# A gMLP value projection by seven block products on two sets of three PSUM banks, with modulation steps moved to the FFN in-projections

## The chip, the cores and the metric

The kernel runs on one core of one Trainium2 chip. The metric is the device time of one execution in microseconds; the time before is the median of three runs.

## The reference

A two-layer generator over 512 latent and 256 context tokens, width 1024. Each layer is FFN, token mixer, FFN; every sublayer is modulated by shift, scale and gate and closed by a LayerNorm over the residual. Layer 0 mixes by a chunked gMLP, layer 1 by attention. What the change touches is the gMLP's `v` and the modulation:

```python
def modulation(cond, w_mod, b_mod):            # 9 vectors of 1024 per layer and condition
    m = jax.nn.silu(cond) @ w_mod + b_mod
    return jnp.split(m[..., None, :], N_MOD, axis=-1)

def ffn_sublayer(x, shift, scale, gate, w_in, w_out, ln_g, ln_b):
    y = swiglu(modulate(x, shift, scale), w_in, w_out)
    return layer_norm(ALPHA * x + 0.5 * gate * y, ln_g, ln_b)

def gmlp_mix(h, w_in, sgu_g, sgu_b, w_s, b_s, w_out):       # h: 768 x 1024, w_in: 1024 x 6144
    b_, t_, _ = h.shape
    u, v = jnp.split(jax.nn.gelu(h @ w_in, approximate=False), 2, axis=-1)
    v = layer_norm(v, sgu_g, sgu_b)
    v = v.reshape(b_, t_ // CHUNK, CHUNK, GMLP_GROUPS, GMLP_HALF // GMLP_GROUPS)
    v = jnp.einsum('gpq,bnqgc->bnpgc', w_s, v) + b_s.T[None, None, :, :, None]
    return (u * v.reshape(b_, t_, GMLP_HALF)) @ w_out
```

Both conditions (latent and context) need the modulation vectors, save the last four of layer 1, which only the latent tokens use.

## The kernel before

*Stages.* One instruction stream per engine runs six sublayers one after another: the first FFN (to about 540 us of the profiled execution), the gMLP (to 1190: the v projection from 555.97 to 753.86, then u with the spatial gate, then the out-projection), the second FFN (to 1698), the third, of layer 1 (to 2200), attention, and the last FFN on the latent tokens. The 768 tokens are six blocks of 128.

*Products.* Every operand is split into two fp32r parts, high and low, and a product is three matmuls: high by high, high by low, low by high. The FFN in-projections work on half the tokens (three blocks) and half the width at a time and take seven such block products where eight are the plain count (`tile_strassen`, L1024; matmuls 128x384). Their stationary operands are the boxes `comb` named B11, B21, T1, T2, T3, B22, T4: B11 and B21 are the two halves of the width of blocks 0 to 2, B22 belongs to blocks 3 to 5, the T are differences. `combine` (L670) makes all but the first two in pieces, between the first products of a sublayer. Sums of weights are made on DVE ahead of the split (`units`, L304).

*The v projection before* is plain: `gmlp` (L1217) calls `token_proj` (L1172) for six chunks of 512 columns; each takes 8 slices of the width by 6 blocks by 3, 864 matmuls of 128x512 in all, in six banks. `evacuate` then runs gelu on ACT, `bn_stats` on DVE and a DMA to `v_spill` on POOL's queue.

*Weights.* `weight_order` (L207) lists all pieces of 256 KB in the order of use. `load_raw` (L277) issues them on SP's queue as one of six raw tiles comes free. ACT casts a piece to its high part, DVE subtracts for the low one (`split_later` L170, `flush` L175); up to eight split pieces wait (`w`), and `pump` (L347) decides how many are prepared at a slot between products.

*Modulation.* `mod_unit` (L387) makes one of the 18 vectors in 16 steps (two halves of 512 columns, eight slices of the width). A step takes a raw piece `mraw` of 256 KB (SP, three tiles) and runs one DVE `scalar_tensor_tensor` per condition into `acc`. After the eighth step of a half, POOL runs a `partition_all_reduce` (L410) and a DMA that adds the row in DRAM (L411), once per condition. `MOD_PLAN` (L69) says which vectors belong to which sublayer; `fill` (L526) runs one step at a slot of the products, and `fill_pair` (L538) two where there is one condition. What is left when the slots are over is run at once at the start of `End.begin` (L1941), which closes a sublayer. In the FFN's in-projection, tiles from `OPENED` on have one `fill_pair`, every fourth two.

*The closing.* In the last products of an out-projection, block after block is finished: DVE adds and `bn_aggr` to `ve`, POOL raises it to the power -1/2 (`rs`, L203), DVE makes `nb`, ACT the normalised `z`. PE transposes block b-2 after six of the 18 matmuls of block b, so block 0 is turned while block 2 is multiplied. PE, like each engine, runs its instructions in the order written.

Of the kernel before, what the change touches and what calls it, by code (L numbers as in the profile page):

```python
# [7 lines left out]
F32 = mybir.dt.float32  # L8
F32R = mybir.dt.float32r
AF = mybir.ActivationFunctionType  # L10
# [59 lines left out]
    [(0, 2), (0, 3), (0, 4)],  # L70
    [(0, 5), (0, 6), (0, 7), (0, 8), (1, 0), (1, 1)],
    [(1, 2), (1, 3)],
    [(1, 4), (1, 5), (1, 6), (1, 7)],
# [20 lines left out]
class Backbone:  # L94
# [112 lines left out]
    def weight_order(self):  # L207
# [96 lines left out]
    def units(self, jobs):  # L304
        dve, w = self.dve, None
        for kind, srcs in jobs:
            if kind == "u":
                for _ in srcs:
                    w = self.unit_of(self.take())
                    self.drop(1)  # L310
                    yield w
                continue
            g1 = self.take()
# [31 lines left out]
            yield w  # L345

# [323 lines left out]
    def combine(self):  # L670
# [14 lines left out]
        h1, h2, t1, t4 = [], [], [], []  # L685
        for n in range(HALF):
            b = HALF + n
            banks = [self.h_transposes(b, half) for half in range(int(begun is not None), 2)]
            h2.append(cut(self.z[b][:, 512:1024]))
            if begun:  # L690
                h1.append(begun[n][0])
                t1.append(begun[n][1])
            else:
                h1.append(cut(self.z[b][:, 0:512]))
                self.h_affine(b, 0, banks[0], False, h1[n])
            self.h_affine(b, 1, banks[-1], not begun, h2[n])
# [12 lines left out]
            low("T2", n, t2)  # L709
            if n and not begun:  # L710
                yield
        for name in ("T3",) if begun else ("T1", "T3"):
            self.new_comb(name)
        if not begun:
# [5 lines left out]
            high("T1", 2, t1[2])  # L720
        sub(h1[0], h2[0], h1[0])
# [360 lines left out]
    def ffn(self, l, i, nblocks, end, prev):  # L1082
# [133 lines left out]

    def gmlp(self, l, i, nblocks, end, prev):  # L1217
# [5 lines left out]
        vbox = self.box("v", F32)  # L1223
# [25 lines left out]
        for cc in range(CC):  # L1249

            def evacuate(b, ps):
                v = self.q(512)
                self.act.activation(v, ps, AF.Gelu)
                self.dve.bn_stats(vst[b][:, cc], v)
                nc.gpsimd.dma_start(spill[cc][b * P : b * P + P, :], v)
# [578 lines left out]
    def body(self):  # L1834
# [11 lines left out]
            (self.gmlp, 0, 3, NB, "c"),  # L1846
# [259 lines left out]
```

## Time and profile before

| | us |
|---|---|
| median of three runs (lowest, highest) | 2812.37 (2812.07, 2812.89) |
| the profiled execution, by its own time | 2812.64 |
| span of its instructions | 2810.9 |
| mean granted TensorE clock | 0.998 |
| v projection, in the span | 555.97 to 753.86 |

The page of the profile gives, engine by engine, busy time with its share of the span; then the span in forty equal slices; DMA queues; the chain of work that ended last; and groups of instructions. A row of a timeline reads: start, duration in us, engine, source line, operation, output<-inputs, and in brackets how long the engine was idle before it and which instruction released it. PE is matmul, PEld its weight load, DVE the vector engine, ACT the scalar engine, POOL GpSimd.

### The profile page before, as it was taken

The numbers are of one execution on the slowest core, as the hardware profiler recorded it, in microseconds if no ns is written. First come the engines' busy times: TensorE is split into PE (matmuls) and PEld (weight loads), VectorE is DVE, ScalarE is ACT, GpSimd is POOL, SyncE is SP. The second block draws the span as 40 slices with busy tenths as digits, with TensorE's granted clock in tenths as the row PEclk, the third lists the DMA queues.
The fourth block names the chain that finished last, engine by engine and source line by source line (L and its number), as shares of the span: only waits on it lengthen the run. The fifth ranks groups of instructions, "written<-read, shape, count | busy, mean of one in ns | idle before, by whom it ended". The sixth has DMA issues, their size and how long they took to land.

```text
span 2810.9 us, 40763 instructions
## 1 busy us (share of the span) xinstructions
PE 2768.7 (98%) x14478; PEld 2502.6 (89%) x14478; DVE 2009.0 (71%) x3483; ACT 1245.8 (44%) x2467; POOL 535.2 (19%) x605
## 2 busy tenths in 40 slices
PE   7999999999999999999999999999999999999998
PEld 5999988888899988899999889999988888888886
DVE  6867779587687786687777758777786698733445
ACT  6544432432355532474444237444432666623321
POOL 1001044233311232200102220001242121000001
PEclk9999999999999999999999999999999999999999
DMA  7444366355555464344346534443584524454352
GB/s 232 141 129 123 111 233 202 120 196 195 190 174 165 154 233 144 124 149 143 110 126 204 180 113 131 144 131 116 163 308 154 147 70 89 134 150 132 111 168 82
DMA packets 398820, 430.00 MB, mean 153 GB/s; under 512 B 28504, under 2 KB 288024, under 8 KB 398616
## 3 DMA queue, kind: packets, MB, share of 16 engines
q1 hardware_dynamic: 364504, 319.40, 36.5%
q0 software_dynamic: 34112, 108.00, 12.4%
q8 instruction: 113, 1.85, 0.3%
q14 instruction: 91, 0.75, 0.1%
HBM read 366.10 MB, written 63.41 MB: 153 GB/s over the span
## 4 chain that ended last, share of the span: by engine, by line
PE 65%; ACT 2%; issue 2%; DVE 2%; POOL 1%; DMA 0%; DVEq 0%; POOLq 0%; ACTq 0%; SPq 0%
PE ps L89 64%; PE pp L89 1%; POOL acc L410 0%; ACT z L2004 0%; POOL rs L203 0%; ACT h L628 0%; ACT p L1519 0%; DVE z L89 0%; DVE nm L1511 0%; ACT w L172 0%; ACT comb L642 0%; ACT p L1522 0%; ACT pT L166 0%; POOL zhat L2006 0%; DVE pT L167 0%
## 5 line engine op out<-in xcount | busy, mean ns | idle before, releaser
L89 PE MATMUL ps<-comb,w 128*128 128x384 f32 x5544 | 969.5, 335 | 6.5 <-ACT w L172 3.0
L89 PEld LDWEIGHTS ps<-comb,w 128*128 128x128 f32 x5544 | 961.5, 188 | 10.3 <-DVE w L89 3.8
L89 PE MATMUL ps<-w,acts 128*128 128x512 f32 (+1 forms) x3792 | 860.1, 388 | 0.0
L89 PEld LDWEIGHTS ps<-w,acts 128*128 128x128 f32 x3792 | 707.3, 188 | 145.0
L89 ACT CAST w<-raw 128x512 fp32r<-128x512 f32 x630 | 388.1, 621 | 750.7 <-PE ps L89 657.3
L89 DVE TENSOR_TENSOR w<-raw,w 128x512 fp32r<-128x512 f32 x630 | 459.7, 737 | 313.1 <-ACT w L89 312.2
L89 PE MATMUL ps<-h,w 128*128 128x384 f32 (+2 forms) x2304 | 445.1, 353 | 0.2 <-DVE w L173 0.2
L89 PEld LDWEIGHTS ps<-h,w 128*128 128x128 f32 x2304 | 402.4, 188 | 37.8 <-DVE w L173 0.4
L89 DVE SCALAR_TENSOR_TENSOR acc<-mraw,cs,acc 128x512 f32<-128x512 f32 x378 | 281.4, 778 | 21.0 <-DMA mraw<-in_w_mod_dram 20.5
L89 PE MATMUL ps<-w,h 128*128 128x512 f32 x1200 | 274.6, 390 | 0.0
L410 POOL PARTITION_ALL_REDUCE acc<-acc x56 | 202.7, 3627 | 350.5 <-DVE acc L89 309.2
L89 PEld LDWEIGHTS ps<-w,h 128*128 128x128 f32 x1200 | 224.6, 188 | 46.3
L89 POOL DMA_DIRECT2D act<-stage x84 | 48.0, 571 | 981.1 <-DVE stage L89 950.9
L89 POOL DMA_DIRECT2D q<-act x226 | 128.7, 624 | 456.7 <-DVE acts L89 315.5
L89 DVE TENSOR_TENSOR w<-sums,w 128x512 fp32r<-128x512 f32 x198 | 135.8, 687 | 75.8 <-ACT w L89 75.7
L89 ACT COPY q<-ps 128x384 f32<-128x384 f32 x179 | 86.1, 481 | 205.3 <-PE ps L89 202.0
L89 DVE TENSOR_TENSOR acts<-q,acts 128x384 fp32r<-128x384 f32 (+1 forms) x262 | 146.5, 595 | 9.3 <-ACT acts L89 9.2
L89 ACT CAST acts<-q 128x384 fp32r<-128x384 f32 (+1 forms) x262 | 126.4, 519 | 49.9 <-DMA q<-act 33.9
L89 ACT CAST w<-sums 128x512 fp32r<-128x512 f32 x198 | 122.7, 621 | 31.2 <-DVE sums L323 18.6
L173 DVE TENSOR_TENSOR w<-raw,w 128x512 fp32r<-128x512 f32 x114 | 75.7, 687 | 27.9 <-ACT w L172 27.2
L203 POOL TENSOR_TENSOR rs<-ve,mhalf 128x1 f32<-128x1 f32 (+3 forms) x47 | 39.0, 829 | 273.1 <-DVE ve L200 167.8
L172 ACT CAST w<-raw 128x512 fp32r<-128x512 f32 x114 | 68.2, 632 | 47.3 <-PE ps L89 27.0
(208 smaller groups left out, 2221.6 us busy)
## 6 DMA issues: line engine op xcount, KB each, us to landing
raw<-in_ffn_w_in_dram SPq DMA_DIRECT2D x400, 256.0 KB
mraw<-in_w_mod_dram SPq DMA_DIRECT2D x256, 256.0 KB
raw<-in_ffn_w_out_dram SPq DMA_DIRECT2D x176, 256.0 KB
q<-act POOLq DMA_DIRECT2D x216, 192.0 KB, 4.2
act<-stage POOLq DMA_DIRECT2D x74, 384.0 KB, 3.1
raw<-in_gmlp_w_in_dram SPq DMA_DIRECT2D x96, 256.0 KB
zhat<-z POOLq DMA_DIRECT2D x26, 512.0 KB, 2.9
raw<-in_gmlp_w_out_dram SPq DMA_DIRECT2D x48, 256.0 KB
```

Source lines behind the costliest of these rows:

```text
L89: return self.tc.keep_in_program_order(f(*args, **kwargs))
L172: self.act.copy(hi, src)
L173: self.lows.append((key, lambda: self.dve.tensor_tensor(lo, src, hi.bitcast(F32), ALU.subtract)))
L203: self.last_rstd = self.nc.gpsimd.tensor_tensor(rs, ve, self.mhalf[:, 0:1].to_broadcast([P, n]), ALU.pow).ins
L410: nc.gpsimd.partition_all_reduce(accs[c], accs[c], P, bass_isa.ReduceOp.add)
```

## The change

The v projection becomes `gmlp_v`: the six chunks of columns are taken as three pairs, each pair by seven block products (three blocks by half the width by 512 columns; the products T1, T2, T3, B22, T4 and two more, 36 matmuls of 128x512 each), in two sets of three PSUM banks that take turns. `weight_order` lists its pieces in quads; the new `units_of_pair` forms the sums of weights on DVE. The gMLP is now planned as kind "s", so the FFN before it hands over blocks 0 to 2 as B11 and B21 and `combine` makes the rest while the v stage opens; it also writes the first halves of blocks 3 to 5 to DRAM (`kept`), from which B12 is made for the u projection, which takes its operands from the four boxes. No modulation step runs in the v stage any more: `MOD_PLAN` is divided anew, and the tiles of the FFN in-projections from `OPENED` on take two `fill_pair` each.

```diff
 MOD_PLAN = [
-    [(0, 2), (0, 3), (0, 4)],
-    [(0, 5), (0, 6), (0, 7), (0, 8), (1, 0), (1, 1)],
-    [(1, 2), (1, 3)],
-    [(1, 4), (1, 5), (1, 6), (1, 7)],
+    [(0, 2), (0, 3), (0, 4), (0, 5)],
+    [(0, 6), (0, 7), (0, 8)],
+    [(1, 0), (1, 1), (1, 2)],
+    [(1, 3), (1, 4), (1, 5), (1, 6), (1, 7)],
     [],
     [(1, 8)],
 ]
...
-        for cc in range(GMLP_HALF // 512):
-            o = GMLP_HALF + cc * 512
-            jobs.append(("u", [wi[k * P : k * P + P, o : o + 512] for k in range(KD)]))
+        quad = lambda cc, half: [
+            wi[k * P : k * P + P, GMLP_HALF + cc * 512 : GMLP_HALF + cc * 512 + 512]
+            for k in range(4 * half, 4 * half + 4)
+        ]
+        each = lambda *qs: [s for group in zip(*qs) for s in group]
+        jobs.append(("u", quad(0, 0) + quad(2, 0) + quad(0, 1) + quad(2, 1)))
+        for a in (0, 2, 4):
+            g1, g2, u1, u2 = quad(a, 0), quad(a, 1), quad(a + 1, 0), quad(a + 1, 1)
+            if a < 4:
+                jobs.append(("vr", each(u1, u2, g1) + each(g1, u1) + g2 + u2))
+            else:
+                jobs.append(("vs", g1 + each(u1, u2) + g1 + g2 + each(g1, u1) + g2 + u2))
...
+            if kind[0] == "v":
+                yield from self.units_of_pair(kind == "vr")
...
+    def units_of_pair(self, opened):
+
+        def of_raw():
+            for _ in range(4):
+                w = self.unit_of(self.take())
+                self.drop(1)
+                yield w
+
+        def settled(w):
+            if any(key is w for key, _ in self.lows):
+                self.flush()
+
...
+            s1 = [self.acc() for _ in range(4)]
+            for k in range(4):
+                u1, u2, g1 = self.take(), self.take(), self.take()
+                self.dve.tensor_tensor(s1[k], u1, u2, ALU.add)
+                self.dve.tensor_tensor(held[k], s1[k], g1, ALU.subtract)
+                units.append(self.unit_of(held[k]))
+                self.drop(3)
+                yield units[k]
+            for k in range(4):
+                yield self.unit_of(s1[k])
...
-    def combine(self):
+    def combine(self, keep=False):
...
+                if keep:
+                    self.pool.dma_start(self.kept[n], self.z[b][:, 0:512])
...
-        for name in ("T3",) if begun else ("T1", "T3"):
-            self.new_comb(name)
+        if not begun:
+            self.new_comb("T1")
...
-            self.tile_strassen(lambda: acts.place(f), opened, int(f >= OPENED) * (1 + int(f % 4 == 0)))
+            self.tile_strassen(lambda: acts.place(f), opened, int(f >= OPENED) * 2)
...
+    def gmlp_v(self, room, spill, vst, early_group, late_group):
...
+        self.combining = self.combine(True)
+        sets = [[self.bank(("v", x, t)) for t in range(HALF)] for x in range(2)]
...
+        def finish(cc, b, v):
+            dve.bn_stats(vst[b][:, cc], v)
+            self.nc.gpsimd.dma_start(spill[cc][b * P : b * P + P, :], v)
+
+        def out(cc, b, src):
+            v = self.q(512)
+            act.activation(v, src, AF.Gelu)
+            after.append(lambda: finish(cc, b, v))
...
+        def slot():
+            self.flush()
+            waiting = after[:]
+            after.clear()
+            if todo:
+                todo.pop(0)()
+            elif later:
+                later.pop(0)()
+            if self.combining is not None:
+                self.pump(max(0, min(2, LEAD - len(self.wready))))
+                if next(self.combining, self) is self:
+                    self.combining = None
+            else:
+                self.pump(2)
+            for f in waiting:
+                f()
+
+        def step(x, name, go_on, evacuate):
+            kw = dict(skip_group_check=True) if go_on else {}
+            for k in range(4):
+                (w,) = self.weights(1)
+                while name not in self.made:
+                    next(self.combining, None)
+                c = self.comb[name]
+                for t in range(HALF):
+                    ps, s = sets[x][t], slice(t * P, t * P + P)
+                    self.mm(ps, c[:, 0, k, s], w[:, 0], not go_on and k == 0, False, **kw)
+                    self.mm(ps, c[:, 0, k, s], w[:, 1], False, False, **kw)
+                    self.mm(ps, c[:, 1, k, s], w[:, 0], False, k == 3, **kw)
+                if k == 3:
+                    assert not todo
+                    todo.extend(lambda t=t: evacuate(t, sets[x][t]) for t in range(HALF))
+                slot()
+                self.release(1)
...
+                u2 = zs()
+                step(x, "T2", True, lambda t, ps: act.copy(u2[t], ps))
+                p5 = ms()
+
+                def keep5(t, ps):
+                    act.copy(p5[t], ps)
+                    act.copy(ps, u2[t])
+
+                step(y, "T1", False, keep5)
+            step(x, "T3", True, lambda t, ps: summed(a + 1, HALF + t, ps, p5[t]))
+
+            def third(t, ps):
+                summed(a, HALF + t, ps, p5[t])
+                if tail_seed:
+                    act.copy(ps, tail_seed[t])
+
+            step(y, "B22", True, third)
+            if a == 4:
+                late_group()
+                assert not later
+            step(x, "T4", True, lambda t, ps: out(a + 1, t, ps))
...
+        step(0, "B11", False, lambda t, ps: act.copy(first[t], ps))
+        step(1, "B11", False, lambda t, ps: act.copy(first[3 + t], ps))
+
+        def opened(t, ps):
+            out(0, t, ps)
+            act.copy(ps, first[t])
+
+        step(0, "B21", True, opened)
+        step(1, "B21", True, lambda t, ps: out(2, t, ps))
+        rest(0, 0, first[0:3], first[3:6])
+        rest(1, 2, first[3:6], None)
+        early_group()
+        rest(0, 4, None, None)
...
-            if not cc:
-                self.filler_raw()
-            if cc == CC - 1:
-                load_ws(0)
-                following = group(0)
-                next(following)
-                self.later(4, lambda: next(following))
-            self.pin(cc > 0)
-            self.token_proj(range(NB), evacuate)
...
+        self.gmlp_v(vbox_all, spill, vst, begin_group, lambda: next(self.following))
...
-                self.in_proj(ps, ws, slice(x * HT, x * HT + HT))
+                parts = [self.comb[name] for name in (("B11", "B21"), ("B12", "B22"))[x]]
...
-            (self.gmlp, 0, 3, NB, "c"),
+            (self.gmlp, 0, 3, NB, "s"),
```

Three places in the order of the instructions. In the names, `acc` is a modulation accumulator (in the v stage also a sum of two weight pieces), `mraw` a raw piece of `w_mod`, `cs` the conditioning column, `held` a difference of weight pieces, `vst` the statistics of v, `w` and `raw` split and raw weights, `acts` the FFN's or gMLP's activations, `q` scratch.

First, DVE near the end of the gMLP's out-projection, up to the first instruction of the closing (L778 before, L852 after). Before:

```order
L89 SCALAR_TENSOR_TENSOR acc<-mraw,cs,acc 128x512 x2
L89 TENSOR_TENSOR w<-raw,w 128x512
L89 TENSOR_TENSOR acts<-q,acts 128x384 x2
L89 TENSOR_TENSOR w<-raw,w 128x512
L89 TENSOR_TENSOR acts<-q,acts 128x384 x2
L89 TENSOR_TENSOR w<-raw,w 128x512 x2
L778 SCALAR_TENSOR_TENSOR q<-ps,gate 128x512
```

And after:

```order
L89 TENSOR_TENSOR w<-raw,w 128x512
L89 TENSOR_TENSOR acts<-q,acts 128x384 x2
L89 SCALAR_TENSOR_TENSOR acc<-mraw,cs,acc 128x512 x2
L89 TENSOR_TENSOR w<-raw,w 128x512
L89 SCALAR_TENSOR_TENSOR acc<-mraw,cs,acc 128x512 x2
L471 SCALAR_TENSOR_TENSOR acc<-mraw,cs,acc 128x512 x4
L89 TENSOR_TENSOR w<-raw,w 128x512
L471 SCALAR_TENSOR_TENSOR acc<-mraw,cs,acc 128x512 x2
L852 SCALAR_TENSOR_TENSOR q<-ps,gate 128x512
```

Three steps of the last vector (two accumulations each) stand now in `End.begin`, among and behind the last weight lows; before, the last step stood ahead of the last four of them.

POOL at the same place, before:

```order
L410 ISA acc<-acc 128x512
L411 DMA mod_10000<-acc 16x1x32
L410 ISA acc<-acc 128x512
L411 DMA mod_10000<-acc 16x1x32
L203 ISA
L203 TENSOR_TENSOR rs_11177<-ve_11176,mhalf 128x1
L2006 DMA zhat_0_11146<-z 128x1024
L203 TENSOR_TENSOR rs_11209<-ve_11208,mhalf 128x1
```

And after:

```order
L479 ISA acc<-acc 128x512
L480 DMA mod_10508<-acc 16x1x32
L479 ISA acc<-acc 128x512
L480 DMA mod_10508<-acc 16x1x32
L203 ISA
L203 TENSOR_TENSOR rs_11297<-ve_11296,mhalf 128x1
L203 TENSOR_TENSOR rs_11329<-ve_11328,mhalf 128x1
L2217 DMA zhat_0_11266<-z 128x1024
```

The two all-reduces and their DMAs stand directly ahead of the first `rs` in both; what has moved is the DVE work that they follow.

Second, DVE at the end of the second FFN's out-projection, before:

```order
L89 TENSOR_TENSOR w<-raw,w 128x512
L89 TENSOR_TENSOR acts<-q,acts 128x384 x2
L89 TENSOR_TENSOR w<-raw,w 128x512
L89 TENSOR_TENSOR acts<-q,acts 128x384 x2
L89 TENSOR_TENSOR w<-raw,w 128x512 x2
L778 SCALAR_TENSOR_TENSOR q<-ps,gate 128x512
```

And after:

```order
L89 TENSOR_TENSOR w<-raw,w 128x512
L89 TENSOR_TENSOR acts<-q,acts 128x384 x2
L89 SCALAR_TENSOR_TENSOR acc<-mraw,cs,acc 128x512 x2
L89 TENSOR_TENSOR w<-raw,w 128x512
L89 SCALAR_TENSOR_TENSOR acc<-mraw,cs,acc 128x512 x2
L471 SCALAR_TENSOR_TENSOR acc<-mraw,cs,acc 128x512 x2
L89 TENSOR_TENSOR w<-raw,w 128x512
L852 SCALAR_TENSOR_TENSOR q<-ps,gate 128x512
```

One step (two conditions) is left for the closing here; before there was none. The end of the third FFN has the same with one condition.

Third, DVE at the opening of the v stage, before:

```order
L778 SCALAR_TENSOR_TENSOR q<-ps,gate 128x512
L173 TENSOR_TENSOR w<-raw,w 128x512 x6
L789 TENSOR_TENSOR z<-z,q 128x512
L644 TENSOR_TENSOR h<-q,h 128x4x128
L794 BN_STATS st<-z 128x6
L644 TENSOR_TENSOR h<-q,h 128x4x128
L755 BN_AGGR mv<-st 128x2
```

And after, where the first sums of weights meet the end of `combine`:

```order
L89 TENSOR_TENSOR comb<-z,comb 128x4x128 x2
L89 BN_STATS vst_5535<-q 128x6
L89 TENSOR_TENSOR w<-raw,w 128x512
L89 TENSOR_TENSOR acc<-raw 128x512
L89 TENSOR_TENSOR held<-acc,raw 128x512
L89 TENSOR_TENSOR comb<-z,comb 128x4x128 x2
L89 BN_STATS vst_5536<-q 128x6
L89 TENSOR_TENSOR w<-held,w 128x512
L89 TENSOR_TENSOR acc<-raw 128x512
L89 TENSOR_TENSOR held<-acc,raw 128x512
L89 TENSOR_TENSOR comb<-t_5615,comb 128x4x128
L89 BN_STATS vst_5537<-q 128x6
```

Between the statistics of the first outputs there are now two differences of `comb` and two sums of weights for each piece.

More of the change, by code (lines that the diff above doesn't have):

```diff
@@ L312, in units @@
                 continue
+            if kind[0] == "v":
+                yield from self.units_of_pair(kind == "vr")
+                continue
             g1 = self.take()
@@ L345, in units @@
             yield w
+    def units_of_pair(self, opened):
[7 more added lines that the diff above has]
+                self.flush()
+        held = self.main.tile([P, 4, 512], F32, tag="gate", bufs=1, name="held")
+        held = [held[:, k] for k in range(4)]
+        units = []
+        if opened:
+            s1 = [self.acc() for _ in range(4)]
[9 more added lines that the diff above has]
+        else:
+            yield from of_raw()
+            for k in range(4):
+                u1, u2 = self.take(), self.take()
+                self.dve.tensor_tensor(held[k], u1, u2, ALU.add)
+                units.append(self.unit_of(held[k]))
+                self.drop(2)
+                yield units[k]
+            for k in range(4):
+                g1 = self.take()
+                settled(units[k])
+                self.dve.tensor_tensor(held[k], held[k], g1, ALU.subtract)
+                units[k] = self.unit_of(held[k])
+                self.drop(1)
+                yield units[k]
+            yield from of_raw()
+        for k in range(4):
+            g1, u1 = self.take(), self.take()
+            self.dve.tensor_tensor(u1, g1, u1, ALU.subtract)
+            w = self.unit_of(u1)
+            self.drop(2)
+            yield w
+        for k in range(4):
+            g2 = self.take()
+            settled(units[k])
+            self.dve.tensor_tensor(held[k], g2, held[k], ALU.subtract)
+            w = self.unit_of(held[k])
+            self.drop(1)
+            yield w
+        yield from of_raw()
     def pump(self, most=9):
@@ L685, in combine @@
         h1, h2, t1, t4 = [], [], [], []
+        if keep:
+            self.kept = self.dram.tile([HALF, P, 512], F32, name="kept")
         for n in range(HALF):
@@ L720, in combine @@
             high("T1", 2, t1[2])
+        self.new_comb("T3")
         sub(h1[0], h2[0], h1[0])
@@ L1247, in group, with begin_group @@
             yield wT, r, bs
[L1249 to L1255, printed above, removed]
-            if not cc:
-                self.filler_raw()
-            if cc == CC - 1:
-                load_ws(0)
-                following = group(0)
-                next(following)
-                self.later(4, lambda: next(following))
-            self.pin(cc > 0)
-            self.token_proj(range(NB), evacuate)
+        def begin_group():
+            load_ws(0)
+            self.following = group(0)
+            next(self.following)
+        self.gmlp_v(vbox_all, spill, vst, begin_group, lambda: next(self.following))
+        following = self.following
         self.pin(False)
@@ L1321, in project @@
             for x, ps in enumerate(banks):
-                self.in_proj(ps, ws, slice(x * HT, x * HT + HT))
+                parts = [self.comb[name] for name in (("B11", "B21"), ("B12", "B22"))[x]]
+                for k in range(KD):
+                    w, c, kk = ws[k // 4], parts[k // 4], k % 4
+                    s = slice(kk * P, kk * P + P)
+                    self.mm(ps, w[:, 0, s], c[:, 0, kk], k == 0, False)
+                    self.mm(ps, w[:, 0, s], c[:, 1, kk], False, False)
+                    self.mm(ps, w[:, 1, s], c[:, 0, kk], False, k == KD - 1)
             self.release(2)
```

52 lines of the change are left out of this document (51 added, 1 removed).

## The prediction

> **What bounds the kernel now.** I read the page from the top (busy shares, slices), then stretches of the stage that is rewritten, then each engine in order of time at the ends of the sublayers, where the change moves work.
>
> ```profile
> span 2810.9 us, 40763 instructions
> PE 2768.7 (98%) x14478; PEld 2502.6 (89%) x14478; DVE 2009.0 (71%) x3483; ACT 1245.8 (44%) x2467; POOL 535.2 (19%) x605
> GB/s 232 141 129 123 111 233 202 120 196 195 190 174 165 154 233 144 124 149 143 110 126 204 180 113 131 144 131 116 163 308 154 147 70 89 134 150 132 111 168 82
> ...
> core 0: us, PE busy (x) PEld busy (x) DVE busy (x) ACT busy (x) POOL busy (x), PEclk, DMA share, GB/s
> 555.97:753.86 197.89, 197.89 (x884) 163.98 (x882) 152.62 (x218) 65.78 (x115) 74.75 (x69) 1.00 0.58 190
> ```
>
> PE is busy 98% of the span, and without a gap in the v projection (the last row: us, busy and count per engine, granted clock, DMA). So a matmul taken out there is worth its whole spacing, and a wait put in front of PE anywhere costs its whole length. The v stage holds 864 products of 128x512 and two groups of eight transposes of some 0.8 each: (197.89 - 1.6) / 864 = 0.227 us a product.
>
> **The change, part by part.** *Products.* 21 block products of 36 instead of 24: 108 x 0.227 = **-24.5 us**. Clock and shape of the matmul stay, so this has one answer. The u projection issues as many as before.
>
> *Mod steps in the FFN in-projections.* Tiles from 8 on get two pairs of steps instead of one in each of three FFNs; before, every fourth tile had two.
>
> ```profile
> 1311.70:1326.40 14.70, 14.70 (x87) 14.70 (x86) 9.48 (x17) 6.67 (x13) 1.57 (x3) 1.00 0.54 164
> 1326.40:1341.10 14.70, 14.70 (x86) 14.70 (x85) 12.03 (x20) 6.58 (x13) 0.58 (x1) 1.00 0.50 145
> 1149.44 1.40 DVE L89 SCALAR_TENSOR_TENSOR acc<-mraw,cs,acc 128x512 f32<-128x512 f32 x2
> ```
>
> In two tile-long stretches around a two-pair tile DVE is busy 9.5 and 12.0 of 14.7 us; one more pair (1.4) fits, and PE had no gap there: 0. Their 256 KB loads add 16 KB/us at most, their SP waits already stand in these tiles: 0. If that cover were gone, 10 tiles in three FFNs would each lose up to 1.4: the far bound is 42, which I drop because two-pair tiles show no gap.
>
> *Opening of the v stage.* The FFN end now hands over blocks 0 to 2 alone, as between two FFNs, and combine runs during the first four products. The FFN that opens at 1190 is the nearest row.
>
> ```profile
> 1190.56 2.27 PE L89 MATMUL ps<-comb,w 128*128 128x384 f32 x12
> 1201.78 2.38 PE L89 MATMUL ps<-comb,w 128*128 128x384 f32 x12 [0.54 <-DVE w L89]
> 1204.86 2.04 PE L89 MATMUL ps<-comb,w 128*128 128x384 f32 x10 [0.70 <-DVE w L89]
> ...
> 1223.55 0.69 DVE L320 TENSOR_TENSOR sums<-raw 128x512 f32<-128x512 f32 x1
> 1224.27 0.69 DVE L323 TENSOR_TENSOR sums<-sums,raw 128x512 f32<-128x512 f32 x1
> 1224.88 1.29 DVE L89 TENSOR_TENSOR comb<-z,comb 128x512 fp32r<-128x512 f32 x2
> 1226.08 0.68 DVE L89 TENSOR_TENSOR w<-sums,w 128x512 fp32r<-128x512 f32 x1
> ```
>
> PE waits 1.24 there for weight lows; the v units are a little shorter: **+1.4**. DVE works without pause (an instruction each 0.60) and has the first summed weight at 1226.8. In the v stage two more bn_stats stand ahead of it: 1228.0. PE wants it at 1190.56 + 4 x 36 x 0.227 + 2.4 (transposes) + 1.4 = 1227.1: 0.9 late. The next three summed weights cost DVE 5, 5 and 4 instructions (3.0, 3.0, 2.4 us), PE 9 x 0.227 = 2.04: 0.95, 0.95 and 0.4 more. **+3.2**; bounds 0 (the scheduler's order hides it) and 8 (loads late as well). In the later pairs the same burst has up to seven weights of lead, 14 us, against a shortfall of 3: 0.
>
> *From v to u.* All-reduces leave the v stage, and with them a reload on POOL.
>
> ```profile
> 754.95 0.54 POOL L1255 DMA_DIRECT2D v_spill<-q  x1 [0.15 <-issue]
> 762.62 1.37 POOL L203 TENSOR_TENSOR rs<-ve,mhalf 128x6 f32<-128x6 f32 x1 [7.13 <-issue]
> 774.67 0.74 PE L89 MATMUL ps<-w_sT,vn 128*128 128x256 f32 x4 [1.38 <-ACT su L89]
> ```
>
> POOL's first rstd after all-reduces starts 7.1 us after the instruction ahead of it, though nothing in the profile held it. Without that the norm of v comes some 3 us sooner, and PE's wait of 1.38 for an ACT that was late by it goes: **-1.4** (to +2, since three gelus now follow the last product and the first mod load of the u stage is cold).
>
> *The ends of three sublayers.* Here the moved steps hurt. The slots of gMLP, of the second FFN and of the third no longer hold all their steps: 3, 1 and 1 are left and run at once when the closing begins, each followed by its all-reduces, the reload and only then the rstd of block 0. Before, the last steps came at the 15th, 11th and an early enough turn.
>
> ```profile
> 1150.28 3.66 POOL L410 PARTITION_ALL_REDUCE acc<-acc  x1 [3.93 <-DVE acc L89]
> 1154.24 0.82 POOL L411 DMA_DIRECT2D mod<-acc  x1 [0.30 <-POOL acc L410]
> 1154.82 3.46 POOL L410 PARTITION_ALL_REDUCE acc<-acc  x1
> 1158.58 0.80 POOL L411 DMA_DIRECT2D mod<-acc  x1 [0.30 <-POOL acc L410]
> 1170.30 0.60 POOL L203 TENSOR_TENSOR rs<-ve,mhalf 128x1 f32<-128x1 f32 x1 [10.93 <-DVE ve L200]
> 1171.13 1.24 ACT L2004 ACTIVATE z<-z,nb,rs 128x1024 f32<-128x1024 f32 x1 [6.95 <-DVE nb L760]
> 1172.88 1.03 PE L89 MATMUL ps<-ident,z 128*128 128x128 f32 x8
> ...
> 1160.13 0.69 DVE L89 TENSOR_TENSOR w<-raw,w 128x512 fp32r<-128x512 f32 x1 [1.36 <-ACT w L89]
> 1164.21 0.69 DVE L89 TENSOR_TENSOR w<-raw,w 128x512 fp32r<-128x512 f32 x1 [3.39 <-ACT w L89]
> ...
> 1667.74 0.69 DVE L89 TENSOR_TENSOR w<-raw,w 128x512 fp32r<-128x512 f32 x1 [2.14 <-ACT w L89]
> 1680.49 1.03 PE L89 MATMUL ps<-ident,z 128*128 128x128 f32 x8
> 2175.34 0.69 DVE L89 TENSOR_TENSOR w<-raw,w 128x512 fp32r<-128x512 f32 x1 [2.45 <-ACT w L89]
> 2188.49 1.03 PE L89 MATMUL ps<-ident,z 128*128 128x128 f32 x8
> ```
>
> From the start of the first of two all-reduces to the end of the second's DMA issue is 9.1 us (1150.28 to 1159.38), the reload 7.1, from rstd to the normalised block 2.1 (1170.30 to 1172.37): 18.3 until PE can turn block 0, which it did at 1172.88. Queued behind the late rstd are nb on DVE, z on ACT and, in order, all of PE. In gMLP the step of the 18th turn follows the weight low of 1160.13; with three more pairs of 1.4 and the low of 1164.21 between them, the first accumulator is done at 1166.3: PE turns at 1184.6, **+11.7**. In the second FFN (two conditions, one step left) it is 1667.74 + 0.69 + 1.4 + 0.7 = 1670.5: 1688.8 against 1680.49, **+8.3**. In the third (one condition, one all-reduce: 4.8 + 7.1 + 2.1 = 14.0) 2175.34 + 0.69 + 1.4 + 0.7 = 2178.1: 2192.1 against 2188.49, **+3.6**. Bounds: loads of the last steps late by 2.6 (longer), a reload of 6.4 instead of 7.1 (shorter), as when POOL goes the other way:
>
> ```profile
> 257.24 0.54 POOL L89 DMA_DIRECT2D act<-stage  x1 [14.36 <-DVE stage L89]
> 264.22 6.72 POOL L410 PARTITION_ALL_REDUCE acc<-acc  x2 [6.43 <-DVE sums L320]
> ```
>
> together 19 to 28, taken 23.6. [...]
>
> *The clock after a stall.*
>
> ```profile
> 47.83:51.24 3.41, 1.24 (x7) 0.47 (x5) 2.53 (x5) 3.41 (x10) 0.00 (x0) 1.00 0.81 229
> 51.24:54.65 3.41, 3.25 (x10) 3.25 (x11) 3.41 (x7) 2.56 (x6) 0.00 (x0) 0.50 0.54 155
> ```
>
> After a window of 3.41 us in which PE was busy for 1.24, the next ran at clock 0.50: 1.7 us lost. After 11.7 and 8.3 us idle PE resumes at half clock for the rest of a window and, half the time, one more: 1.7 each; the third stall drops it about every second time, 0.9. **+4.3**, bounds 1 and 8. [...]
>
> *Sum*, against the profiled execution's 2812.64: -24.5 + 1.4 + 3.2 - 1.4 + 23.6 + 4.3 = +6.6, so 2819.2. That execution stands 0.27 over the median, which gives **2819.0**.
>
> **Rivals.** (1) *The all-reduces still fit* (faster). Decided by when the first of the two starts: at least 18.3 us ahead of PE's turn of block 0 nothing is lost; before it had 22.6 (1150.28 to 1172.88). For it speaks that DVE is idle 3.4 us in that stretch and might run the steps ahead of my places; against it, the new order has them behind the last weight low, and POOL cannot start without them. It takes away 23.6 and 4.3: 2791.1.
> (2) *The v stage is fed too slowly.* The summed weights of a pair's first product need 12 loads of 256 KB in 8.2 us, 384 GB/s, over the 308 of the busiest slice, and DVE 3.0 us for 2.04 of PE. If the lead is not there in the two later bursts, PE loses 4 x 0.95 in each, and in-order DVE holds back the bank adds behind it, as much again: +15, 2834. Against it: the stage had 58% of DMA and DVE at 152.6 of 197.9.
> (3) *Only the longest end stalls*, since POOL or the loads get to the single steps sooner: 8.3, 3.6 and 2.6 of clock go: 2804.5.
>
> **How the numbers follow.** The main case 0.62 (own range 2810 to 2828: opening 0 to 6, ends 21 to 26, clock 1 to 7), (1) 0.14, (2) 0.12, (3) 0.12. 2802 to 2836 leaves out (1) and the tails of (2) and of the main case. 0.2%, about what a measurement of this kernel tells from no change, is 5.6 us: faster means under 2806.7, which (1) and most of (3) give, 0.22; slower means over 2818.0, (2) and somewhat over half of the main case, 0.48; between them 0.30.
>
> **What would show it.** Right: some 756 products in a v stage of about 176 us; PE waiting 10 to 13, 7 to 9 and 3 to 5 us ahead of the transposes of block 0 at three ends, in the chain behind POOL's rs; clock windows of 0.50 behind them; a first gap of about 4 us where T2 opens. Wrong: rs on time at the ends (then it is faster by over 20), or gaps in the later pairs or in the FFN tiles (then slower).

## The result, and the profile after

The changed kernel takes 2837.24 us (median of four runs, 2835.5 to 2838.96), the kernel before 2812.63 in the same comparison: ratio 1.0087, 95% interval 1.007 to 1.0105. It is slower by 24.6 us. Forecast was slower, by 6.6 us, to 2819.0, with a range up to 2836; the measured time lies 1.2 us beyond it. The profiled execution took 2835.5.

From the page of the changed kernel: span and busy shares.

```profile
span 2833.7 us, 41057 instructions
PE 2756.2 (97%) x14370; PEld 2487.9 (88%) x14370; DVE 2085.7 (74%) x3613; ACT 1290.6 (46%) x2556; POOL 533.3 (19%) x608
```

PE has 108 matmuls less and 12.5 us less to do, and the span is 22.8 us longer: some 35 us more in which PE is idle. The row of the v stage, and PE's rows where it waited longest (start, duration, and in brackets the idle time ahead with its releaser):

```profile
553.96:741.13 187.17, 178.76 (x783) 144.93 (x781) 143.66 (x239) 110.05 (x200) 21.70 (x40) 0.99 0.65 214
...
593.38 2.49 PE L89 MATMUL ps<-w,comb 128*128 128x512 f32 x9 [1.25 <-DVE w L89]
639.27 0.96 PE L89 MATMUL ps<-w,comb 128*128 128x512 f32 x3 [1.50 <-ACT ps L89]
642.63 7.59 PE L89 MATMUL ps<-w,comb 128*128 128x512 f32 x25 [2.40 <-ACT ps L89]
761.94 0.74 PE L89 MATMUL ps<-w_sT,vn 128*128 128x256 f32 x4 [1.38 <-ACT su L89]
1175.04 1.97 PE L89 MATMUL ps<-ident,z 128*128 128x128 f32 x8 [14.63 <-ACT z L2215]
1693.51 1.97 PE L89 MATMUL ps<-ident,z 128*128 128x128 f32 x8 [8.62 <-ACT z L2215]
2207.02 1.97 PE L89 MATMUL ps<-ident,z 128*128 128x128 f32 x8 [3.86 <-ACT z L2215]
2259.89 0.20 PE L89 MATMUL ps<-ident,s 16*128 16x16 f32 x1 [2.17 <-DMA s<-mod]
```

The v stage is 187 us; the prediction gave about 176 as a sign of being right, though the terms of its own sum come to 178 (197.9 - 24.5 + 1.4 + 3.2). At the three ends PE waits 14.6, 8.6 and 3.9 us for the normalised block 0, and in attention 2.2 for a modulation row. What holds block 0 in the gMLP:

```profile
1154.87 3.66 POOL L479 PARTITION_ALL_REDUCE acc<-acc  x1 [12.50 <-DVE acc L471]
1160.28 0.82 POOL L480 DMA_DIRECT2D mod<-acc  x1 [1.75 <-issue]
1160.85 3.46 POOL L479 PARTITION_ALL_REDUCE acc<-acc  x1
1164.61 0.80 POOL L480 DMA_DIRECT2D mod<-acc  x1 [0.30 <-POOL acc L479]
1172.93 1.12 POOL L203 TENSOR_TENSOR rs<-ve,mhalf 128x1 f32<-128x1 f32 x2 [7.52 <-issue]
1173.55 0.16 DVE L834 SCALAR_TENSOR_TENSOR nb<-mv,rs 128x1 f32<-128x1 f32 x1 [11.82 <-POOL rs L203]
1173.75 2.37 ACT L2215 ACTIVATE z<-z,nb,rs 128x1024 f32<-128x1024 f32 x2 [22.19 <-DVE nb L834]
```

The first all-reduce starts when DVE is through with the leftover steps; 20.2 us later PE turns block 0. Ahead of `rs` POOL has no row for 7.52 us, and for 7.54 and 6.86 at the other two ends (`rs` at 1691.40 and 2204.91). In the prediction such a stretch goes by the name of reload; what POOL does in it no view shows.

Lengths of the stages in us, each from the start of PE's first matmul of it to that of the next; the ends run from the out-projection to the next in-projection. The last three columns belong to experiments told below. (The edge of 555.97 given above for the kernel before lies 0.08 us in front of its first v matmul.)

| stage | before | after | drain_late | free_ends | best |
|---|---|---|---|---|---|
| start of the v stage | 556.05 | 553.96 | 555.16 | 556.83 | 558.02 |
| v | 197.81 | 187.17 | 187.96 | 187.98 | 182.27 |
| u, spatial | 238.11 | 237.82 | 237.78 | 238.03 | 240.91 |
| gMLP end | 198.59 | 215.95 | 199.80 | 198.98 | 198.99 |
| second FFN, in | 325.32 | 324.84 | 333.15 | 325.38 | 325.43 |
| second FFN, end | 182.29 | 193.77 | 182.68 | 182.70 | 182.69 |
| third FFN, in | 324.91 | 324.50 | 332.94 | 325.40 | 325.79 |
| third FFN, end | 183.97 | 189.21 | 183.56 | 186.72 | 183.56 |
| attention | 228.34 | 232.62 | 237.06 | 228.51 | 229.18 |

### The profile page after: what moved, and what is told of

The parts are those of the page before. It is cut to its first block, busy times and chain, and to the rows that moved or that the text cites. A ratio compares the mean times of both kernels' runs of the same rounds, so it can differ in the third digit from the quotient of the medians.

```text
span 2833.7 us, 41057 instructions
## 1 busy us (share of the span) xinstructions
PE 2756.2 (97%) x14370; PEld 2487.9 (88%) x14370; DVE 2085.7 (74%) x3613; ACT 1290.6 (46%) x2556; POOL 533.3 (19%) x608
## 4 chain that ended last, share of the span: by engine, by line
PE 65%; issue 3%; DVE 2%; ACT 2%; POOL 1%; DMA 1%; DVEq 0%; POOLq 0%; SPq 0%; ACTq 0%
PE ps L89 64%; PE pp L89 1%; DMA mraw<-in_w_mod_dram 0%; POOL acc L479 0%; ACT z L2215 0%; ACT p L1730 0%; DVE z L89 0%; POOL rs L203 0%; DVE nm L1722 0%; DVE acts L89 0%; ACT h L697 0%; DVE acc L89 0%; ACT w L172 0%; ACT p L1733 0%; ACT pT L166 0%
## 5 line engine op out<-in xcount | busy, mean ns | idle before, releaser
L89 PE MATMUL ps<-comb,w 128*128 128x384 f32 x6696 | 1172.9, 335 | 5.0 <-ACT w L172 1.9
L89 PEld LDWEIGHTS ps<-comb,w 128*128 128x128 f32 x6696 | 1160.8, 188 | 8.4 <-ACT ps L89 2.4
L89 ACT CAST w<-raw 128x512 fp32r<-128x512 f32 x643 | 395.3, 621 | 650.5 <-PE ps L89 543.4
L89 DVE SCALAR_TENSOR_TENSOR acc<-mraw,cs,acc 128x512 f32<-128x512 f32 x383 | 274.3, 750 | 10.7 <-DMA mraw<-in_w_mod_dram 10.5
L89 PE MATMUL ps<-h,w 128*128 128x512 f32 (+1 forms) x1152 | 241.4, 372 | 0.2 <-DVE w L173 0.2
L89 PEld LDWEIGHTS ps<-h,w 128*128 128x128 f32 x1152 | 203.3, 188 | 37.7 <-DVE w L173 0.4
L89 PE MATMUL ps<-w,comb 128*128 128x512 f32 x756 | 176.8, 394 | 6.8 <-ACT ps L89 3.9
L89 PEld LDWEIGHTS ps<-w,comb 128*128 128x128 f32 x756 | 142.2, 189 | 39.9 <-ACT ps L89 4.8
L89 DVE TENSOR_TENSOR q<-q,ps 128x384 f32<-128x384 f32 (+1 forms) x69 | 39.6, 575 | 61.3 <-PE ps L89 61.2
L203 POOL TENSOR_TENSOR rs<-ve,mhalf 128x1 f32<-128x1 f32 (+3 forms) x47 | 38.5, 819 | 235.5 <-DVE ve L200 109.7
```

The lines of the kernel that those rows point to most:

```text
L89: return self.tc.keep_in_program_order(f(*args, **kwargs))
L203: self.last_rstd = self.nc.gpsimd.tensor_tensor(rs, ve, self.mhalf[:, 0:1].to_broadcast([P, n]), ALU.pow).ins
```

## The experiments

Two theories were set against each other: (A) the all-reduces and the stretch without a row on POOL ahead of `rs` (7.52 us) make the three stalls, wherever the steps come from; (B) the late DVE steps and their loads hold the closing. For the v stage: (D) seeds that wait behind sums of weights.

**drain_late.** The leftover steps are run behind the last `rs` of the closing:

```diff
     def begin(self, nblocks):
         k = self.k
-        for _ in k.filler:
-            pass
         if self.nxt is None:
+            for _ in k.filler:
+                pass
             rows = k.box("rows", F32)
...
         (self.last if self.nxt is None else self.inner)(nblocks, close)
+        with self.k.behind():
+            for _ in self.k.filler:
+                pass
```

> The changed kernel with one edit: the mod steps left over are run behind the last rs of the closing instead of ahead of the first. By its order DVE keeps the accumulations at their old places (ahead of the first closing product); only POOL's all-reduces and their DMAs now stand behind the sixth rs. Theory A (POOL's all-reduces and its reload in front of rs stall PE at three ends, 14.6 + 8.6 + 3.9 us in the trace of the changed kernel, and 6.3 us of half clock follow): 33 us less, about 2804, PE turning block 0 without a gap over 1 us. Rival B (the late DVE steps and the loads that they wait for hold the closing): the gaps stay within 3 us of what they were, 2830 to 2837.

Measured 2825.7, ratio 1.0045 (1.0032 to 1.0058). The ends lose 33 us against the changed kernel and stand within 1.3 us of their lengths before the change (table), while DVE's accumulations keep the places of the changed kernel (the last of the gMLP start 175.1 us into its out-projection in both): theory A holds for the ends, and B falls. The total is in neither forecast, A's 2804 or B's 2830 to 2837, since 21 us came back elsewhere: 8.3 and 8.4 us in the two in-projections that follow, and 4.4 in attention. DVE and POOL as the second FFN opens, and what PE waits for:

```profile
1192.04 3.53 POOL L479 PARTITION_ALL_REDUCE acc<-acc  x1 [5.99 <-issue]
1196.84 3.50 POOL L479 PARTITION_ALL_REDUCE acc<-acc  x1
1191.18 0.68 DVE L89 TENSOR_TENSOR w<-raw,w 128x512 fp32r<-128x512 f32 x1
1192.38 2.73 DVE L89 TENSOR_TENSOR comb<-q,comb 128x512 fp32r<-128x512 f32 x1
1195.04 1.36 DVE L89 TENSOR_SCALAR z<-ps,modA,modB 128x128 f32<-128x128 f32 x4
1196.32 3.57 DVE L89 TENSOR_TENSOR w<-raw,w 128x512 fp32r<-128x512 f32 x1
1199.94 3.57 PE L89 MATMUL ps<-comb,w 128*128 128x384 f32 x10 [5.67 <-DVE w L89]
```

A DVE instruction of 0.68 takes 2.73 and 3.57 beside an all-reduce, and each ends 0.45 us ahead of that all-reduce's end: these two last until POOL is nearly through. PE waits for the weight low behind it.

**before_left.** The kernel before, with its last 3, 1 and 1 steps kept back by a count in `fill`:

```diff
+        self.left = 16 * len(MOD_PLAN[n]) - (0, 3, 1, 1, -99, -99)[n]
...
-                next(self.filler, None)
+                if self.left > 0:
+                    self.left -= 1
+                    next(self.filler, None)
```

> The kernel before with one edit: the last 3, 1 and 1 mod steps of the gMLP, the second and the third FFN are kept back for the closing, as many as the changed kernel has there. The v projection is the old one. Theory A: the stalls come with the steps alone, +27 us of gaps, +6 of half clock, and +4 in attention if the late columns of layer 1 cause the 2.17 us gap there: 2845 to 2850. Rival C (the stalls need the denser loads or the earlier closing of the new v stage): under +15, below 2828.

Measured 2815.03, ratio 1.0011 (1.0002 to 1.002): A's forecast fails, and the number lies in C's range (under 2828). C's reason does not follow from it, since the run did not make the steps late; that steps left over must run late was taken for granted.

```profile
1142.99 3.66 POOL L410 PARTITION_ALL_REDUCE acc<-acc  x1 [1.24 <-DVE acc L402]
1169.68 0.60 POOL L203 TENSOR_TENSOR rs<-ve,mhalf 128x1 f32<-128x1 f32 x1 [16.86 <-DVE ve L200]
1172.25 1.03 PE L89 MATMUL ps<-ident,z 128*128 128x128 f32 x8
...
2238.52 0.20 PE L89 MATMUL ps<-ident,s 16*128 16x16 f32 x1 [2.08 <-DMA s<-mod]
```

Kept back for slots that ran nothing, the steps had their raw pieces long since, the order put them ahead of the last weight lows, and the first all-reduce starts 26.7 us ahead of `rs`. Nothing stalls. The wait of 2.08 in attention does come: with the last vector of layer 1 closed only by `End.begin`, its columns are read in attention.

**before_skip.** So the same steps were made late in another way: the first six slots of the gMLP and of the second FFN run none, and the pieces then arrive as late as in the changed kernel.

```diff
+SKIP = (0, 6, 6, 0, 0, 0)
...
+                if self.skip > 0:
+                    self.skip -= 1
+                else:
+                    next(self.filler, None)
```

> The kernel before with one edit: the first six fill slots of the gMLP and of the second FFN run no mod step, so that 3 steps and 1 step are left at their closings and each raw piece arrives as late as in the changed kernel; DVE's order at the gMLP's end is then the changed kernel's, row for row. Theory A2 (what decides is when the first all-reduce starts: in the run with steps kept back it started 26.7 us ahead of rs and nothing stalled; the new v projection has no part in it): gaps of 13 to 15 and 8 to 9 us ahead of the transposes of block 0 and some 6 us behind them, +29, about 2841. Rival C (it needs the new v stage): no gap over 3 us, under 2820.

Measured 2846.88, ratio 1.0121 (1.0107 to 1.0135), 34 us above the kernel before, where A2 had said 29 and C under 8.

```profile
777.17 0.58 PE L91 MATMUL ps<-w_sT,vn 128*128 128x256 f32 x1 [5.86 <-ACT vn L168]
1195.29 1.97 PE L91 MATMUL ps<-ident,z 128*128 128x128 f32 x8 [12.58 <-ACT z L2010]
1712.74 1.97 PE L91 MATMUL ps<-ident,z 128*128 128x128 f32 x8 [8.07 <-ACT z L2010]
```

The two stalls come in the old kernel (12.6 where 13 to 15 was expected, and 8.1), 26 us with what follows them at the two ends. The new v projection has no part in them. A third, unforeseen one of 5.86 stands between v and u: the shift put a pair of all-reduces ahead of the norm of v, the same chain at a fourth place.

**small_reduce.** What is the price of the 7.52 us ahead of `rs`, apart from the all-reduces? In the steps left for the closing only 16 of 512 columns are summed (the others stay unsummed):

```diff
-                nc.gpsimd.partition_all_reduce(accs[c], accs[c], P, bass_isa.ReduceOp.add)
+                part = accs[c][:, 0:16] if self.draining else accs[c]
+                nc.gpsimd.partition_all_reduce(part, part, P, bass_isa.ReduceOp.add)
```

> The changed kernel, but the steps left for the three closings sum only 16 of their 512 columns over the partitions; the other columns of these vectors are left unsummed. [...] If a small all-reduce takes under 1 us, the three gaps shrink by 5 to 6, 5 to 6 and 2.5 to 3.5 us, to 9, 3 and under 1.5: 2818 to 2824. Rival G (an all-reduce has a fixed price whatever its columns): less than 1 us off each gap, 2834 to 2837.

Measured 2820.93, ratio 1.003 (1.0019 to 1.0042), inside the forecast 2818 to 2824.

```profile
1156.44 0.88 POOL L480 PARTITION_ALL_REDUCE acc<-acc  x1 [12.75 <-DVE acc L471]
1159.64 0.69 POOL L480 PARTITION_ALL_REDUCE acc<-acc  x1
1160.63 0.78 POOL L481 DMA_DIRECT2D mod<-acc  x1 [0.30 <-POOL acc L480]
1168.15 1.12 POOL L203 TENSOR_TENSOR rs<-ve,mhalf 128x1 f32<-128x1 f32 x2 [6.74 <-issue]
1170.26 1.97 PE L89 MATMUL ps<-ident,z 128*128 128x128 f32 x8 [8.53 <-ACT z L2218]
```

The all-reduces shrink from 3.66 and 3.46 to 0.88 and 0.69, and the first stall by 6.1 us to 8.5; the others go to 2.8 and 2.3 (the third forecast under 1.5). Ahead of `rs` 6.74 us stay that no row fills, where 7.52 stood behind the large all-reduces; the order has the ISA instruction of `rs`'s line there. So this stretch is a price of its own, about half of the first stall; what goes on in it no view shows.

**seeds.** In the v stage the product B22 ends with three bank adds on DVE, after each of which ACT copies the next pair's seed into the bank. They were issued in three slots, between sums of weights; now in one:

```diff
             def third(t, ps):
-                summed(a, HALF + t, ps, p5[t])
-                if tail_seed:
-                    act.copy(ps, tail_seed[t])
+                if not tail_seed:
+                    summed(a, HALF + t, ps, p5[t])
+                elif not t:
+                    for n in range(HALF):
+                        summed(a, HALF + n, sets[y][n], p5[n])
+                    for n in range(HALF):
+                        act.copy(sets[y][n], tail_seed[n])
```

> The changed kernel with one edit in the v stage: in the two pairs that are followed by another, the three bank adds of the product B22 and the three copies that seed its banks are issued in one slot instead of three. Theory D (the gaps of 1.50 and 2.40 us ahead of the second pair's T2 are PE waiting for seeds whose DVE adds stand behind sums of weights, and the half-clock window behind them costs 1.7): 4 to 5.6 us less, 2831 to 2833. Rival E (DVE has not the throughput there, the summed weights come late instead): gaps of the same sum on DVE w, within 1 us of 2837.

Measured 2834.95, ratio 1.008 (1.0067 to 1.0094), 2.3 under the changed kernel: between D's 2831 to 2833 and E's 2836 to 2838, in neither. The trace shows D's mechanism, and where the rest of its gain went. DVE there in the changed kernel, and then with the edit:

```profile
637.39 0.68 DVE L89 TENSOR_TENSOR q<-ps,p 128x512 f32<-128x512 f32 x1
637.99 0.68 DVE L89 TENSOR_TENSOR acc<-raw 128x512 f32<-128x512 f32 x1
638.71 0.69 DVE L89 TENSOR_TENSOR held<-acc,raw 128x512 f32<-128x512 f32 x1
639.32 0.68 DVE L89 BATCH_NORM_STATS2 vst<-q 128x6 f32<-128x512 f32 x1
640.14 0.69 DVE L89 TENSOR_TENSOR w<-held,w 128x512 fp32r<-128x512 f32 x1
640.75 0.68 DVE L89 TENSOR_TENSOR q<-ps,p 128x512 f32<-128x512 f32 x1
```

```profile
635.20 1.88 DVE L89 TENSOR_TENSOR q<-ps,p 128x512 f32<-128x512 f32 x3
...
760.58 1.23 PE L89 MATMUL ps<-w_sT,vn 128*128 128x256 f32 x4 [3.43 <-ACT su L89]
```

The adds (`q<-ps,p`) stood 3.4 us apart, one to a slot, while PE needs 2.04 for a slot (nine products of 0.227); put together they free the banks in time, the gaps of 1.50 and 2.40 are gone (0.18 is left), with the half-clock window behind them (3.41 us in which the granted clock reads 0.50; the last section has the rows), and the v stage is 181.66, 5.5 shorter. At the start of u 4.9 us came back: from the last gelu to the waiting product 19 us pass in both runs (742.95 to 761.94, 741.73 to 760.58), and PE, sooner through, waits 3.43 there, 2.05 more, and its next 18 matmuls of 128x384 take 5.30 (from 761.61), where 18 such took 3.28 in the changed kernel (from 754.79, ahead of its wait).

**free_ends.** More slots, so that nothing is left for a closing:

```diff
-            self.fill(int(0 < j < GMLP_CH - 1))
+            self.fill(int(0 < j < GMLP_CH - 1) + int(j in (4, 6, 8, 10, 12, 14, 16, 18)))
...
-            self.tile_strassen(lambda: acts.place(f), opened, int(f >= OPENED) * 2)
+            self.tile_strassen(lambda: acts.place(f), opened, int(f >= OPENED) * 2 + int(f > OPENED and f % 2 and i + l > 0))
...
-        step(b2, "B22", True, None, second)
+        step(b2, "B22", True, None, second, int(fills > 2))
```

> The changed kernel with more slots for mod steps: eight more in the gMLP's u stage, a third pair in every other tile from the ninth in the second and third FFN. Nothing is left for a closing, by the order of DVE. Theory A: the three stalls, their clock and the gap in attention go, 37 us less, about 2800. Rival F (the added steps make DVE or the loads late in the u stage and the FFN tiles): some of it comes back as new gaps there, 2806 to 2820.

Measured 2806.5, ratio 0.9978 (0.9969 to 0.9987): 30.7 under the changed kernel, where A had said 37, and at the low end of F's range. The ends and attention are back at their old lengths (table), save the third end, where a gap of 2.44 stands, behind a DVE that waited 2.53 for a late `mraw`: part of F.

```profile
2021.34 3.03 PE L89 MATMUL ps<-w,acts 128*128 128x512 f32 x12 [2.44 <-DVE q L89]
```

With the stalls gone, the new v stage is worth the 9.8 us that the table shows.

**best.** As free_ends with six extra tiles in the second FFN (not seven) and two in the third, with the edit of `seeds` for all pairs, and the stage's last outputs evacuated ahead of the u weights:

```diff
-        while todo or after:
-            slot()
+        self.flush()
+        for f in todo + [None]:
+            for g in after:
+                g()
+            after.clear()
+            if f:
+                f()
```

> Nothing left for the closings (more slots: eight in the u stage, six tiles in the second FFN, two in the third), and in the v stage the bank adds of B22 and their seeds in one slot for all three pairs, the last outputs of the stage evacuated ahead of the u weights. Theories A2 and D: 2806.5 of the run with free ends, less 5.5 in the v stage (as the run with early seeds showed), less 2.4 for the gap at 2021 that the fuller slots made, and the v-to-u wait not over 2.5: 2797 to 2801. Rival H (what the v stage gains comes back at the start of u, since 18.9 us pass from the last gelu to u's first spatial products in both runs): 2801 to 2805.

Measured 2798.77, ratio 0.9952 (0.9939 to 0.9964): faster than both kernels, 13.8 under the one before and 38.5 under the changed one, as A2 and D together had said. H is true too in part: PE waits 2.92 there (762.64), and u is 2.8 us longer than before.

**best_swap.** And in the first pair T1 ahead of T2, with one sum of weights in each product. (In this run u2 of two blocks is copied after T3's first matmuls, so part of that pair's values differ; instructions and shapes are the same.)

```diff
+            elif not a:
+                p5, u2 = ms(), zs()
+                step(y, "T1", False, lambda t, ps: act.copy(p5[t], ps))
...
+                step(x, "T2", True, keep2)
```

> The same, and in the first pair T1 is multiplied ahead of T2, so that each of these weights needs one DVE sum where T2 needed two and T1 none. Theory I (the four gaps at 589 to 603 are DVE, which has 3.1 us of work for a weight of T2 and PE 2.04): these 4.7 us go, 4 us under the kernel without the swap. Rival J (combine's lows for T1 and T2 are late instead, since T1 is made behind T2): gaps of the same size at another place, within 1.5 us of it.

Measured 2801.76, ratio 0.9962 (0.9948 to 0.9976), 3 us above `best`, with intervals that overlap.

```profile
594.21 17.47 PE L89 MATMUL ps<-w,comb 128*128 128x512 f32 x71 [0.52 <-DVE w L89]
617.08 33.13 PE L89 MATMUL ps<-w,comb 128*128 128x512 f32 x136 [5.40 <-ACT zraw L89]
```

Theory I holds for its gaps: of 1.25, 0.64 and 0.65 one of 0.52 stays, with a new one of 0.96 at 576.85. Its 4 us of gain do not come: T3 now follows T2 on the same banks, which ACT has to copy first, and that costs 5.4 in one place; by the order, T1 on the other set had covered it.

## Why the prediction was too low

Its terms against the lengths in the two traces (profiled executions, 2835.5 against 2812.64):

| term | forecast | measured |
|---|---|---|
| 108 products less | -24.5 | -24.5, a product still 0.227 |
| opening of the v stage | +1.4 | +2.0, and 0.8 for eight transposes more |
| sums of the first pair | +3.2 | +4.7 |
| sums of the later pairs | 0 | +4.4, and 1.6 of half clock |
| from v to u | -1.4 | -0.3 |
| three ends with their clock | +27.9 | +34.1 |
| attention | not seen | +4.3 |
| all else | 0 | -4.6 |

The rows of the right column add up to 22.5 of the 22.9; the 0.4 in no row lie in the v stage. Of the -4.6, which by luck made the miss smaller, 2.1 lie ahead of the v stage, where the traces differ by as much among themselves, and 1.6 in the last FFN, which takes 373.4 to 374.1 us in every kernel with the new code and 375.4 to 375.5 in those with the old; no run shows why.

*Right.* The products; the three stalls at their places, by the chain all-reduces, stretch without a row, `rs`, `nb`, `z`: 14.6, 8.6 and 3.9 where 11.7, 8.3 and 3.6 were forecast. Rival (1) failed on the condition that it named, a first all-reduce 18.3 us ahead of PE's turn: here 5.5 (it starts at 1154.87, and PE has nothing more to do from 1160.4). Two experiments stand on the two sides of that condition, 26.7 us ahead of `rs` without a stall, and the old kernel with late steps and the stalls.

*Wrong, largest first.* "In the later pairs the same burst has up to seven weights of lead, 14 us, against a shortfall of 3: 0." The weights had lead enough; the bank adds between them had not. This step failed: the working weighed a burst of DVE work against the queue of weights alone and left out that in-order DVE also frees the banks that PE needs next. Rival (2) had the mechanism in half a sentence, and the single edit of `seeds` shows it: 5.5 us of 9.3 by which the v stage was mis-sized.

The ends were mis-sized by 6.2. Of the gMLP's 2.9 us, the chain took 20.2 instead of 18.3 (the first DMA was issued 1.75 behind its all-reduce where 0.30 was read before, and the stretch without a row was 7.52, not 7.13), and the first all-reduce started 5.5 us ahead of PE's turn, not 6.6. The other two stalls were 0.3 longer each. The rest, 2.7, is clock: PE resumed at 0.50 for 4.46 and 4.81 us,

```profile
1175.04:1179.50 4.46, 4.46 (x15) 3.88 (x16) 0.69 (x1) 4.39 (x10) 1.28 (x2) 0.50 0.60 232
1693.51:1698.32 4.81, 4.81 (x16) 4.13 (x17) 0.85 (x2) 4.24 (x10) 1.58 (x3) 0.50 0.55 215
```

which is 2.2 and 2.4 for windows that were costed at 1.7, an estimate from one window of the kernel before, and the third end, costed at half a window, had a whole one (0.50 from 2206.90 to 2210.32).

Attention stood in no term. A leftover step closes its vector late, and the order carries the reading of its columns as far into the next sublayer; `before_left` shows that wait alone. From v to u the stall was not the norm's lateness: the stretch without a row did go (POOL waited 3.68 for `ve` in place of the 7.13, and the rstd starts 6.9 us after u's first matmul where it started 8.8 after), but the product that waits stands behind the read-back of v and ACT's work on it, 19 us from the last gelu, and waits 1.38 as before.

The range failed for the same reason: the main case's own bounds (2810 to 2828) left the later pairs and attention at nothing, and the upper end had room for rival (2) alone, at 2834, not for its mechanism on top of longer ends, while nearly all terms missed on the same side. What is open: the v stage started 554.0 to 558.0 us into the profiled executions of kernels that are alike up to there, which is as large as some of these terms.

## What to carry to other kernels

Ask of a leftover step not how much work it is but when its last input lands and what has to follow it ahead of the next `rs`: in the old kernel the same steps cost nothing or 12.6 us at one place, by whether the first all-reduce started 29 or 5.5 us ahead of PE's turn of block 0. Where a burst of work goes onto an in-order engine, list everything on that engine which frees a buffer, and compare the spacing of those instructions in the burst with the consumer's own. A saving that is spread over a stage shows at its end as less cover for the fixed chain behind it.

## What the hardware showed that was not expected

*Some DVE instructions lasted longer beside an all-reduce, and one all-reduce beside DVE.* Besides the rows above (0.68 to 2.73 and 3.57), the same at the first closing in the changed kernel, under the all-reduce of 1154.87:

```profile
1156.07 2.02 DVE L863 TENSOR_TENSOR z<-z,q 128x512 f32<-128x512 f32 x1
```

and between v and u in `before_skip`, under one that ran from 761.65:

```profile
762.05 2.10 DVE L202 TENSOR_SCALAR ve<-v_var 128x6 f32<-128x6 f32 x1
```

The first takes 0.69 in `small_reduce` (at 1157.64, between its two small all-reduces), the second 0.17 where no all-reduce runs (at 747.81 in the changed kernel). The DVE instructions above end 0.4 to 1 us ahead of the all-reduce, while five that read `ps` ran back to back, 0.61 each, inside one that took from 1608.64 to 1612.09 in the changed kernel. Not every other one was longer: a `w<-raw,w` at 1606.71 took 0.69 inside the all-reduce of 1604.09 to 1607.75. The other way round, an all-reduce took 5.20, where the one of 1154.87 took 3.66, and DVE's instructions beside it ran at full pace (the last row). Why, no view shows.

```profile
1608.65 3.07 DVE L89 SCALAR_TENSOR_TENSOR q<-ps,gate 128x512 f32<-128x512 f32 x5
510.94 5.20 POOL L479 PARTITION_ALL_REDUCE acc<-acc  x1 [5.26 <-DVE acc L89]
512.02 1.02 DVE L89 TENSOR_TENSOR acts<-q,acts 128x384 fp32r<-128x384 f32 x2
```

*The clock read 0.50 after windows in which PE was partly busy.* Two windows of 3.41 us in the changed kernel and what followed each:

```profile
640.19:643.60 3.41, 1.01 (x5) 0.84 (x5) 2.28 (x4) 2.13 (x5) 0.54 (x1) 1.00 0.90 299
643.60:647.01 3.41, 3.41 (x9) 2.65 (x9) 3.41 (x7) 2.55 (x6) 0.54 (x1) 0.50 0.36 138
2258.11:2261.52 3.41, 1.63 (x7) 1.37 (x8) 1.45 (x6) 0.27 (x1) 0.00 (x0) 1.00 0.66 202
2261.52:2264.93 3.41, 3.41 (x9) 2.65 (x8) 0.69 (x1) 1.22 (x2) 0.00 (x0) 0.50 0.17 45
```

PE was busy for 30% and 48% of them, and the clock read 0.50 in the next. In windows of 3.41 us between 100 and 2750 us of the changed kernel's trace, three more at full clock had 0.50 after them, one at each end of a sublayer, with PE busy for 41% (1159.02), 6% (1684.67) and 0% (2203.50); one with 50% (2319.55) and all with more kept 1.00. In the first 60 us the share does not separate them: one of 38% lost it (46.27), and one of 11% kept it (1.90). So no rule is shown, but at these two places gaps of 2.4 and 2.2 us were followed by 3.41 us at 0.50, some 1.7 more.
